# Fewer filler products in attention, five tied behind the state space stage's last products, and the branch gates' products later in the filler

## The chip, the cores and the metric

One core of a Trainium2 chip runs the kernel. The metric is the device time of one execution in microseconds (us). Three runs of the kernel before gave 1414.95, 1415.39 and 1415.87 us; the median is 1415.39 us.

## What is computed

One layer of an encoder with four mixers side by side, for 1024 tokens of width 1024, all in 32-bit floats. Cut to what matters here:

```python
hn = rms_norm(x, norm_scale)
a_x, a_g, q, k, v, b_g, c_x, c_g, d_x, d_g, merge = split(hn @ w_in)   # ten of width 512, merge of 4096
y_a = rglru_mixer(a_x, ...) * silu(a_g)                # gated linear recurrence, both directions
y_b = neighbourhood_attention(q, k, v, ...) * silu(b_g)
y_c = s5_mixer(c_x, ...) * silu(c_g)                   # complex state space, then gelu and a GLU
y_d = pool_mixer(d_x, ...) * silu(d_g)
gates = sigmoid(merge)                                 # four of width 1024
merged = sum over n of (ys[n] @ w_branch[n]) * gates[n]
x = x + merged @ w_out
x = x + sigmoid(x @ ple_gate) * (p @ ple_proj)
```

## The kernel before

Each big product is made of three: both operands are split into a high part (a rounded copy, by ScalarE, ACT) and a low part (the rest, by VectorE, DVE), and `mm3` (L88) multiplies high by high, low by high and high by low into one PSUM tile. A **piece** of `hn @ w_in` gives 128 columns of z for 512 tokens: 8 blocks of the inner dimension by three, 24 matmuls of 128x512 on TensorE (PE). In the trace these are the matmuls of `hnH` or `hnL` with `wh` or `wl`. A new block of 128 columns serves two pieces and needs one split, `wh` on ACT and `wl` on DVE; a new load of 1 MB (`wr`) serves four.

The program runs in stages: start (norms, the per-layer embedding's product), attention, the state space stage (`s5`, L927), its GLU (`glu`, L1099), the gated recurrence (`lru`), pooling, the merge of the four branches, and the two last products (`final`). The stages up to the recurrence leave PE free at times, and for that there is a **filler**: a generator of 108 pieces (`fill`, made in `run`, L1308), which are handed out in a fixed order of parts. A part is four pieces per 256 columns; it brings a function that consumes the result: `gates` (16 pieces each, a sigmoid on ACT and a write to DRAM), `branch_gate` (8 each, a sigmoid on ACT, a multiplication on DVE into `bgt`, and a write), `pool_part` (8, a copy), `s5_u` (4, a copy).

How much filler each stage gets is set by hand. In `attention` (L382) the loop over units of the rounds calls `next(side)`; from the middle of the second round on `side` is the filler. In the stages behind it `drive` (L188) runs the main generator, adds up what it says of PE and DVE, the latter times a factor of `SC`, and takes a piece whenever PE's sum is the smaller. Between `s5` and `glu` two pieces are taken outright.

This is the order in which the program is written down. The order that the engines run is made by a scheduler, which goes through the written order with a timeline of its own and may bring an instruction forward where its engine would be idle; the pieces' buffers (three for `wh` and `wl`, two for `wr`, in turn) and PSUM tiles bound how far. Each engine then runs its list in order.

The state space stage goes through four batches of 128 channels (`s5_batch`, L937), each in two halves `h`. In a batch DVE makes tables (`Gf`, `Q`, `E`), PE transposes `Gf` into `Gt`, and then for each half: PE's V products (`ps_s<-U,Gt`, L1043), DVE's products with `E` into `vr` and `vi`, four scans into `xs`, products into `Xr` and `Xi`, and PE's Y products (`U,M`, then `Xr,Q` and `Xi,Q`, L1089 and L1091), which ACT copies to `Y`. `vr` and `Xr` are one buffer, so the next half's `vr` waits for the Y products. Behind the last half `Y` goes to DRAM (`ydr`), comes back as `gy`, passes a gelu on ACT and DVE, is split into `ygH` and `ygL`, and GLU's products begin.

The change touches `mm3`, `z_gen` (L157), the loop of `attention`, the two lines of products in `s5_batch`, and `run`. `behind` (L704) is there before: it ties an instruction's place in the order behind another's, with no wait.

Of the kernel before, what the change touches and what calls it, by code (L numbers as in the profile page):

```python
# [24 lines left out]
BANDS = (0, 8, 24, 32)  # L25
SC = (1.15, 1.35, 0.95)
VIDX = (0, 1, 1, 2)


class Kern:  # L30
    def __init__(self, tc, es, ins, out):
# [9 lines left out]
        self.dp = es.enter_context(tc.tile_pool(name="dp", bufs=1, space=DRAM))  # L41
        self.zt = "zz"
        self.gd = {}
        self.sgd = {}
# [43 lines left out]
    def mm3(self, ps, pairs):  # L88

        n = len(pairs)  # L90
        mm = self.nc.tensor.matmul
        for k, (aH, aL, bH, bL) in enumerate(pairs):
            mm(ps, aH, bH, start=(k == 0), stop=False)  # L93
            mm(ps, aH, bL, start=False, stop=False)  # L94
            mm(ps, aL, bH, start=False, stop=(k == n - 1))  # L95

    def tr(self, ps, src, k):
# [59 lines left out]
    def z_gen(self, parts):  # L157
# [15 lines left out]
        for k in range(len(todo)):  # L173
            if k + 1 < len(todo):
                prep(k + 1)
            H, L, ct, f = ready.pop(0)
            for hf in range(2):
                ps = self.ps(self.zt[hf])
                t = slice(hf * 512, hf * 512 + 512)
                self.mm3(ps, [(H[:, k, :], L[:, k, :], self.hnH[k][:, t], self.hnL[k][:, t])  # L180
                              for k in range(8)])
                yield 5.2, 0.55 + (f(ct, hf, ps) or 0.0)
# [199 lines left out]
    def attention(self, ap, fill):  # L382
        nc = self.nc
# [19 lines left out]
        side = self.z_gen([self.s5_u(0)])  # L403
        for rd in range(4):
# [5 lines left out]
            for u, _ in enumerate(self.at_units(ap, rd, qk, bias, vd)):  # L410
                if rd < 2 and side is not fill or u % 4 != 2:
                    next(side, None)
                if rd == 0 and u == 1:
                    raw1 = self.qk_load(1)
                if u == 3:
                    next(prep, None)
                    if rd == 0:
                        side = self.at_z(1, raw1)
                        zq = zq + next(side)
                    if rd == 1:  # L420
                        side = fill
# [515 lines left out]
    def s5_batch(self, sb, ct):  # L937
        nc = self.nc
# [15 lines left out]
        Gt = []  # L954
# [82 lines left out]
        for h in range(2):  # L1037
            gg = slice(h * 4, h * 4 + 4)
            V = []
            for k in range(2):  # L1040
                pv = self.ps("s")
                for g in range(4):
                    nc.tensor.matmul(pv[:, g * 128:g * 128 + 128], Gt[k][:, h * 4 + g, :], U[:, h * 4 + g, :],  # L1043
                                     start=True, stop=True)
                V.append(pv)
# [40 lines left out]
            for g in range(4):  # L1086
                c = slice(g * 128, g * 128 + 128)
                a = h * 4 + g
                nc.tensor.matmul(py[:, c], M[:, a, :], U[:, a, :], start=True, stop=False)  # L1089
                for k in range(2):  # L1090
                    nc.tensor.matmul(py[:, c], Q[k][:, a, 1:9, :].rearrange("p t c -> p (t c)"), X[k][:, c],  # L1091
                                     start=False, stop=(k == 1))
            self.copy_a(Y[:, gg, :], py.rearrange("p (g j) -> p g j", g=4))
# [214 lines left out]
    def run(self):  # L1308
        tc = self.tc
        with tc.tile_pool(name="gzp", bufs=2, reuse_waits="tile") as self.gzp:  # L1310
            fill = self.z_gen([self.s5_u(1), self.branch_gate(2, 3584), self.gates(1), self.branch_gate(0, 512), self.branch_gate(3, 4608), self.branch_gate(1, 2560), self.gates(3), self.gates(2), self.pool_part(), self.gates(0)])
            with tc.tile_pool(name="zp", bufs=1, reuse_waits="tile") as self.zp:
# [3 lines left out]
            self.drive(self.s5(), fill, SC[0])  # L1316
            next(fill)
            next(fill)
            self.zt = "zt"
            self.drive(self.glu(), fill, SC[1])  # L1320
            with tc.tile_pool(name="pu", bufs=1, reuse_waits="tile") as pu:
# [50 lines left out]
```

## Time and profile before

| | |
|---|---|
| three runs, median (lowest to highest) | 1415.39 us (1414.95 to 1415.87) |
| the profiled execution, its own time | 1414.34 us |
| its span, first to last instruction | 1412.5 us |
| PE busy | 1366.8 us, 97% |
| PE's weight loads busy | 1120.5 us, 79% |
| DVE busy | 842.0 us, 60% |
| ACT busy | 559.0 us, 40% |
| mean granted TensorE clock | 0.989 |

The profile is of one execution. The span starts at its first instruction; 1.84 us of the execution's time lie around it. Matmuls are pipelined and their ends are modelled: a matmul of 128x512 is shown with some 0.39 us, and the next one starts 0.23 us behind it, so that a busy PE is not PE at its peak, and the pace is read from starts. The clock is given as a share of 2.4 GHz; it has two levels, 1.00 and 0.50. A wait is put down to what ended it last.

### The profile page before, as it was taken

What the parts mean: (1) busy time and instruction counts of PE and PEld (TensorE: products, weight loads), DVE (VectorE), ACT (ScalarE), POOL (GpSimd) and SP (SyncE); (2) the same over time, 40 slices, a digit from 0 to 9 for tenths busy, and PEclk for the clock granted to TensorE, in tenths of its full rate; (3) what the DMA queues carried; (4) which work ended last, traced back from release to release, by engine and by line L of the source; (5) the groups of instructions that cost most, each with busy time, mean ns of one, the idle gap of its engine ahead of it and who ended that gap; (6) DMA issues with size and microseconds to landing.
All of it is one profiled execution on the core that took longest, in us unless ns stands there. A gap on an engine that the chain in (4) does not pass through costs nothing.

```text
span 1412.5 us, 18099 instructions
## 1 busy us (share of the span) xinstructions
PE 1366.8 (97%) x6876; PEld 1120.5 (79%) x6876; DVE 842.0 (60%) x1593; ACT 559.0 (40%) x861; POOL 19.6 (1%) x79
## 2 busy tenths in 40 slices
PE   8999999999999999999839999999999999999998
PEld 6888888888888878888727777778888888888886
DVE  6373446554369797979757447265457766722332
ACT  6344655878622122221133846747322212211221
POOL 2100000000000000000000000000000000000000
PEclk9999999999999999999959999999999999999999
DMA  9533323244243233332344133231846655324443
GB/s 318 162 92 97 119 68 96 87 125 131 73 121 109 90 114 100 105 95 74 108 134 141 49 120 109 74 105 55 321 167 210 210 197 173 127 97 150 171 141 119
DMA packets 134840, 181.91 MB, mean 129 GB/s; under 512 B 29120, under 2 KB 92632, under 8 KB 134754
## 3 DMA queue, kind: packets, MB, share of 16 engines
q1 hardware_dynamic: 134338, 180.72, 40.1%
q8 instruction: 54, 0.88, 0.3%
q14 instruction: 32, 0.26, 0.1%
q0 software_dynamic: 416, 0.04, 0.0%
HBM read 127.06 MB, written 54.03 MB: 128 GB/s over the span
## 4 chain that ended last, share of the span: by engine, by line
PE 92%; DVE 4%; ACT 2%; DMA 1%; issue 1%; SPq 0%; ACTq 0%
PE ps_z L93 19%; PE ps_z L94 19%; PE ps_z L95 19%; PE ps_t L98 4%; PE ps_t L93 3%; PE ps_t L94 3%; PE ps_t L95 3%; PE ps_s L94 2%; PE ps_o L94 2%; PE ps_s L95 2%; PE ps_o L95 2%; PE ps_s L93 2%; PE ps_o L93 2%; PE ps_o L584 2%; PE ps_s L549 2%; PE ps_s L1091 1%
## 5 line engine op out<-in xcount | busy, mean ns | idle before, releaser
L93 PE MATMUL ps_z<-hnH,wh 128*128 128x512 f32 x736 | 290.8, 395 | 3.8 <-DVE xs L1071 1.8
L95 PE MATMUL ps_z<-hnH,wl 128*128 128x512 f32 x736 | 288.6, 392 | 1.7 <-DVE wl L65 1.7
L94 PE MATMUL ps_z<-hnL,wh 128*128 128x512 f32 x736 | 289.6, 393 | 0.0
L93 PEld LDWEIGHTS ps_z<-hnH,wh 128*128 128x128 f32 x736 | 138.2, 188 | 34.8 <-issue 2.4
L95 PEld LDWEIGHTS ps_z<-hnH,wl 128*128 128x128 f32 x736 | 138.3, 188 | 30.0 <-DVE wl L65 2.1
L94 PEld LDWEIGHTS ps_z<-hnL,wh 128*128 128x128 f32 x736 | 138.3, 188 | 27.6 <-issue 1.2
L65 DVE TENSOR_TENSOR wl<-wr,wh 128x1024 fp32r<-128x1024 f32 x88 | 107.3, 1223 | 83.1 <-ACT wh L81 61.0
L81 ACT ACTIVATE wh<-wr 128x1024 fp32r<-128x1024 f32 x88 | 92.8, 1057 | 113.4 <-PE ps_z L94 66.8
L93 PE MATMUL ps_t<-hnH,wh 128*128 128x512 f32 x224 | 87.9, 393 | 0.0
L94 PE MATMUL ps_t<-hnL,wh 128*128 128x512 f32 x224 | 87.8, 392 | 0.0
L95 PE MATMUL ps_t<-hnH,wl 128*128 128x512 f32 x224 | 87.5, 391 | 0.0
L93 PE MATMUL ps_z<-wh,hnH 128*128 128x512 f32 x192 | 75.6, 395 | 0.3 <-ACT zqk L81 0.3
L94 PE MATMUL ps_z<-wl,hnH 128*128 128x512 f32 x192 | 75.1, 393 | 0.0
L95 PE MATMUL ps_z<-wh,hnL 128*128 128x512 f32 x192 | 74.6, 395 | 0.0
L555 DVE CUSTOM_DVE_ANT_0 sc<-ps_s,bias 128x384 f32<-128x384 f32 x64 | 33.9, 555 | 49.0 <-PE ps_s L549 42.3
L77 ACT ACT_TABLE_LOAD x47 | 60.3, 1283 | 3.8 <-issue 2.9
L95 PE MATMUL ps_z<-wh,mL 128*128 128x512 f32 x128 | 51.0, 398 | 0.0
L94 PE MATMUL ps_o<-myL,wh 128*128 128x512 f32 x128 | 50.5, 395 | 0.0
L95 PE MATMUL ps_o<-myH,wl 128*128 128x512 f32 x128 | 50.5, 395 | 0.0
L93 PE MATMUL ps_s<-myH,wh 128*128 128x512 f32 x128 | 50.5, 395 | 0.0
L95 PE MATMUL ps_s<-myH,wl 128*128 128x512 f32 x128 | 50.5, 395 | 0.0
L93 PE MATMUL ps_o<-myH,wh 128*128 128x512 f32 x128 | 50.5, 394 | 0.0
(382 smaller groups left out, 2590.4 us busy)
## 6 DMA issues: line engine op xcount, KB each, us to landing
wr<-in_w_in_dram SPq DMA_DIRECT2D x32, 1024.0 KB, 5.7
gd<-gz SPq DMA_DIRECT2D x32, 512.0 KB, 3.1
mgt<-gd SPq DMA_DIRECT2D x32, 512.0 KB, 3.6
sg<-bgt SPq DMA_DIRECT2D x16, 512.0 KB, 2.9
my<-yd SPq DMA_DIRECT2D x16, 512.0 KB, 3.5
mbr<-in_w_branch_dram SPq DMA_DIRECT2D x8, 1024.0 KB, 7.1
bias<-E SPq DMA_DIRECT2D x128, 48.0 KB, 2.0
xt<-in_x_dram SPq DMA_DIRECT2D x8, 512.0 KB, 10.0
```

What stands on the lines that cost most here:

```text
L65: self.nc.vector.tensor_tensor(out, a, b, ALU.subtract)
L77: self.nc.scalar.activation(out, a, f, **kw)
L81: return self.nc.scalar.activation(out, a, AF.Copy)
L93: mm(ps, aH, bH, start=(k == 0), stop=False)
L94: mm(ps, aH, bL, start=False, stop=False)
L95: mm(ps, aL, bH, start=False, stop=(k == n - 1))
L98: self.nc.tensor.transpose(ps, src, self.ident[:k, :k])
L549: nc.tensor.matmul(pss[h], q[h][:, qs], km[h][(slice(0, 128),) + ks], start=(p == 0), stop=(p == 1))
L555: nc.vector.tensor_tensor_reduce(sc, pss[h], bias[g][h][:, VIDX[j], :], 1.0, -3e38, ALU.add, ALU.max, mx)
L584: m = self.nc.tensor.matmul(po[64 * h:64 * h + 64, j * 128:j * 128 + 128], vb[:, g + c, j, h * 64:h * 64 + 64], PT[h][:, c * 128:c * 128 + ...
L1091: nc.tensor.matmul(py[:, c], Q[k][:, a, 1:9, :].rearrange("p t c -> p (t c)"), X[k][:, c], start=False, stop=(k == 1))
```

## The change

It changes four things. Attention hands out filler in every other unit wherever its `side` is the filler (before: in three of four). The factor of the state space stage, `SC[0]`, goes from 1.15 to 1.25. Behind `s5`, five pieces are taken outright instead of two; the first matmul of two of them is tied behind the last V product of the last batch, that of the other three behind its last Y product. And in the filler's order of parts, three branch gates (0, 3 and 1) move behind `gates(3)` and `gates(2)`.

```diff
-SC = (1.15, 1.35, 0.95)
+SC = (1.25, 1.35, 0.95)
...
     def mm3(self, ps, pairs):
...
         for k, (aH, aL, bH, bL) in enumerate(pairs):
-            mm(ps, aH, bH, start=(k == 0), stop=False)
+            i = mm(ps, aH, bH, start=(k == 0), stop=False)
+            first = i if k == 0 else first
...
+        return first
...
     def z_gen(self, parts):
...
-                self.mm3(ps, [(H[:, k, :], L[:, k, :], self.hnH[k][:, t], self.hnL[k][:, t])
-                              for k in range(8)])
+                first = self.mm3(ps, [(H[:, k, :], L[:, k, :], self.hnH[k][:, t], self.hnL[k][:, t])
+                                      for k in range(8)])
+                if self.hold is not None:
+                    self.behind(first, self.hold)
                 yield 5.2, 0.55 + (f(ct, hf, ps) or 0.0)
...
     def attention(self, ap, fill):
...
-                if rd < 2 and side is not fill or u % 4 != 2:
+                if side is not fill or u % 2:
                     next(side, None)
...
     def s5_batch(self, sb, ct):
...
-                    nc.tensor.matmul(pv[:, g * 128:g * 128 + 128], Gt[k][:, h * 4 + g, :], U[:, h * 4 + g, :],
-                                     start=True, stop=True)
+                    self.last_v = nc.tensor.matmul(pv[:, g * 128:g * 128 + 128], Gt[k][:, h * 4 + g, :],
+                                                   U[:, h * 4 + g, :], start=True, stop=True)
...
-                    nc.tensor.matmul(py[:, c], Q[k][:, a, 1:9, :].rearrange("p t c -> p (t c)"), X[k][:, c],
-                                     start=False, stop=(k == 1))
+                    self.last_y = nc.tensor.matmul(py[:, c], Q[k][:, a, 1:9, :].rearrange("p t c -> p (t c)"),
+                                                   X[k][:, c], start=False, stop=(k == 1))
...
     def run(self):
...
-            fill = self.z_gen([self.s5_u(1), self.branch_gate(2, 3584), self.gates(1), self.branch_gate(0, 512), self.branch_gate(3, 4608), self.branch_gate(1, 2560), self.gates(3), self.gates(2), self.pool_part(), self.gates(0)])
+            fill = self.z_gen([self.s5_u(1), self.branch_gate(2, 3584), self.gates(1), self.gates(3), self.gates(2),
+                               self.branch_gate(0, 512), self.branch_gate(3, 4608), self.branch_gate(1, 2560),
+                               self.pool_part(), self.gates(0)])
...
             self.drive(self.s5(), fill, SC[0])
-            next(fill)
-            next(fill)
             self.zt = "zt"
+            for self.hold, n in ((self.last_v, 2), (self.last_y, 3)):
+                for _ in range(n):
+                    next(fill)
+            self.hold = None
             self.drive(self.glu(), fill, SC[1])
```

The orders of the engines show where the pieces go. All counts of pieces here are of matmuls of `hnH`, `hnL` with `wh`, `wl`, by 24; there are 120 of them in all, before and after (the filler's 108 and 12 of the state space input and the recurrence). In attention, 24.75 pieces stand ahead of the last value product (`ps_o<-PT,vb`) before and 24.25 after.

On PE, the end of the Y products of the third batch's first half (`Q_5509` before, `Q_5378` after), which is where 61.96 pieces have gone by before and 59.00 after. Before:

```order
L1089 MATMUL ps_s<-U,M 128x128
L1091 MATMUL ps_s<-Xr,Q_5508 128x128
L1091 MATMUL ps_s<-Xi,Q_5509 128x128
L95 MATMUL ps_z<-hnH,wl 128x512
L93 MATMUL ps_z<-hnH,wh 128x512
L94 MATMUL ps_z<-hnL,wh 128x512
L95 MATMUL ps_z<-hnH,wl 128x512
```

and after:

```order
L1094 MATMUL ps_s<-U,M 128x128
L1096 MATMUL ps_s<-Xr,Q_5377 128x128
L1096 MATMUL ps_s<-Xi,Q_5378 128x128
L1048 MATMUL ps_s<-U,Gt_5364 128x128 x4
L1094 MATMUL ps_s<-U,M 128x128
L1096 MATMUL ps_s<-Xr,Q_5377 128x128
L101 MATMUL ps_t<-ident,Gf_5898 128x128 x8
L1096 MATMUL ps_s<-Xi,Q_5378 128x128
```

The filler's matmuls that followed are gone. From here to the last V product of the fourth batch 10.0 pieces stand on PE before and none after; the second half of the third batch and the fourth batch's transposes, `Q,Bb` products and first half follow each other.

On PE, the last V product of the fourth batch, tied to by the first two pieces. Before, the last V product (`Gt_6095`) is followed at once by the last half's Y products; after:

```order
L1096 MATMUL ps_s<-Xi,Q_5968 128x128
L1048 MATMUL ps_s<-U,Gt_5954 128x128 x4
L94 MATMUL ps_t<-hnH,wh 128x512
L96 MATMUL ps_t<-hnL,wh 128x512
L97 MATMUL ps_t<-hnH,wl 128x512
L94 MATMUL ps_t<-hnH,wh 128x512
```

Two pieces now stand between the last V product and the last half's `Xr` product: 61.00 pieces have gone by when the Y products run, where it was 72.00.

On PE, the end of the last Y products. Before, GLU's first products follow:

```order
L1089 MATMUL ps_s<-U,M 128x128
L1091 MATMUL ps_s<-Xr,Q_6108 128x128
L1091 MATMUL ps_s<-Xi,Q_6109 128x128
L93 MATMUL ps_s<-ygH_6634,wh 128x512
L93 MATMUL ps_o<-ygH_6634,wh 128x512
```

and after:

```order
L1094 MATMUL ps_s<-U,M 128x128
L1096 MATMUL ps_s<-Xr,Q_5967 128x128
L1096 MATMUL ps_s<-Xi,Q_5968 128x128
L94 MATMUL ps_t<-hnH,wh 128x512
L96 MATMUL ps_t<-hnL,wh 128x512
L97 MATMUL ps_t<-hnH,wl 128x512
```

Ten pieces, the three tied ones among them, now stand between the last Y product and GLU's first product, which comes when 71.00 have gone by. From GLU's last product on, 48 pieces are left before and 47 after. On DVE, none of the 24 multiplications into `bgt` that stood in the state space stage is left there, and 18 splits `wl` stand in it where there were 21: 17 for 18 up to the third batch's first Xi, one for three behind it.

## Rows read from the trace of the kernel before

**Rows 1.** The page, part 2: busy tenths of 40 slices of 35.3 us, and the granted clock.

```profile
PE   8999999999999999999839999999999999999998
...
DVE  6373446554369797979757447265457766722332
...
PEclk9999999999999999999959999999999999999999
```

**Rows 2.** PE's longest waits: engine, tile, line, what ended them; us, times, longest.

```profile
PE ps_s L93 <- ACT ygH L82: 16.5, 1, 16.5
PE ps_s L1091 <- DVE Xr L65: 9.3, 1, 9.3
```

**Rows 3.** PE's timeline, third batch's Y products, and the gap: start, length, operation, idle before.

```profile
629.37 0.38 PE L1091 MATMUL ps_s<-Xi,Q 128*128 128x128 f32 x2
...
699.48 1.05 PE L1043 MATMUL ps_s<-U,Gt 128*128 128x128 f32 x8
...
711.76 0.80 PE L1091 MATMUL ps_s<-Xr,Q 128*128 128x128 f32 x2 [9.30 <-DVE Xr L65]
...
717.21 0.64 PE L1091 MATMUL ps_s<-Xi,Q 128*128 128x128 f32 x2
734.30 0.79 PE L93 MATMUL ps_s<-ygH,wh 128*128 128x512 f32 x1 [16.45 <-ACT ygH L82]
```

**Rows 4.** Stretches: us, busy PE, PE's weight loads, DVE, ACT, POOL; clock, DMA share, GB/s.

```profile
392.60:626.70 234.10, 231.41 (x1300) 191.53 (x1299) 204.40 (x473) 56.17 (x87) 0.00 (x0) 1.00 0.37 106
626.70:713.20 86.50, 75.08 (x447) 63.07 (x445) 67.53 (x125) 15.08 (x25) 0.00 (x0) 0.95 0.27 81
629.40:700.30 70.90, 70.90 (x430) 59.99 (x428) 55.38 (x105) 15.08 (x25) 0.00 (x0) 1.00 0.31 92
...
734.00:738.40 4.40, 4.10 (x10) 3.00 (x11) 4.38 (x6) 3.33 (x5) 0.00 (x0) 0.50 0.41 148
```

**Rows 5.** PE's timeline, inside a filler piece in the state space stage.

```profile
431.71 0.39 PE L94 MATMUL ps_z<-hnL,wh 128*128 128x512 f32 x1
...
432.39 0.39 PE L94 MATMUL ps_z<-hnL,wh 128*128 128x512 f32 x1
```

**Rows 6.** DVE's waits from 392 to 627 us.

```profile
DVE wl L65 <- ACT wh L81: 7.2, 4, 3.2
DVE vr L59 <- PE ps_s L1091: 5.7, 2, 3.7
DVE bgt L59 <- ACT bgt L77: 4.5, 3, 3.2
...
DVE vt L59 <- PE ps_s L1043: 2.0, 2, 1.6
```

**Rows 7.** DVE's waits from 627 to 714 us, all of them.

```profile
DVE vr L59 <- PE ps_s L1091: 8.7, 2, 4.9
DVE vt L59 <- PE ps_s L1043: 8.0, 2, 4.3
```

**Rows 8.** DVE's timeline, the halves of the third and fourth batch.

```profile
631.57 0.69 DVE L59 TENSOR_TENSOR vr<-ps_s,E 128x512 f32<-128x512 f32 x1 [4.87 <-PE ps_s L1091]
...
637.73 0.69 DVE L59 TENSOR_TENSOR vt<-ps_s,E 128x512 f32<-128x512 f32 x1 [4.33 <-PE ps_s L1043]
...
696.22 0.69 DVE L59 TENSOR_TENSOR vr<-ps_s,E 128x512 f32<-128x512 f32 x1 [3.84 <-PE ps_s L1091]
700.56 0.69 DVE L59 TENSOR_TENSOR vt<-ps_s,E 128x512 f32<-128x512 f32 x1 [3.65 <-PE ps_s L1043]
...
712.47 0.69 DVE L62 TENSOR_TENSOR Xi<-Xi,vt 128x512 f32<-128x512 f32 x1
```

**Rows 9.** DVE's groups from 392 to 627 us: busy us, mean ns, idle before them.

```profile
L65 DVE TENSOR_TENSOR wl<-wr,wh 128x1024 fp32r<-128x1024 f32 x18 | 22.0, 1222 | 7.4 <-ACT wh L81 7.2
L59 DVE TENSOR_TENSOR bgt<-bgt,ps_z 128x512 f32<-128x512 f32 x24 | 16.4, 682 | 4.5 <-ACT bgt L77 4.5
```

**Rows 10.** ACT's timeline, the last copy of Y products.

```profile
717.88 0.60 ACT L81 ACTIVATE Y<-ps_s 128x512 f32<-128x512 f32 x1 [17.61 <-PE ps_s L1091]
```

More of the change, by code (lines that the diff above doesn't have):

```diff
@@ L1316, in run @@
             self.drive(self.s5(), fill, SC[0])
-            next(fill)
-            next(fill)
             self.zt = "zt"
+            for self.hold, n in ((self.last_v, 2), (self.last_y, 3)):
+                for _ in range(n):
+                    next(fill)
+            self.hold = None
             self.drive(self.glu(), fill, SC[1])
```

## The prediction

> **What bounds the kernel now.** I read the page first. In 40 slices PE is at 9 nearly everywhere; one slice, the twenty-first, shows 3, and the granted clock 5 of 10 there [rows 1]. So PE's work sets the time, and little but that one hole can be won. Who PE waits for comes next [rows 2]: 16.5 us before the first product of the gate behind the state space stage (GLU for short), for ygH; 9.3 us before the state space stage's last Y products, for Xr. PE's timeline there [rows 3] shows the order of events: the last V product at 699.48, the last half's Y products from 711.76 to 717.85 (0.43 us from one instruction to the next), then nothing until 734.30. The stretches [rows 4] give the clock: 0.50 from 734 to 738.4, where ten matmuls took 4.1 us, so behind the gap PE is at 1.2 GHz, having done nothing for 16 us. A filler piece fills PE for 24 matmuls; three take 0.68 us from start to start [rows 5], so a piece is 5.44 us. Five pieces are 27.2 us, and the two waits together 25.8 us: the size of the change's idea is right.
>
> But what stands ahead of the hole matters more. Up to the third batch's first half DVE is at work 204.40 of 234.10 us while PE shows 231.41 [rows 4]; both are nearly full there. What DVE waits for in it is small and mixed [rows 6]: 5.7 us before vr and 2.0 us before vt, for PE; 7.2 us and 4.5 us before the filler's own wl and bgt, for ACT. Behind that point it waits only before vr and vt, 8.7 and 8.0 us in two halves' turns [rows 7].
>
> **What the orders say.** Not what the code's numbers suggest. In attention the order holds half a piece less than before, not five: what attention no longer asks for, the scheduler brings forward from the state space stage. The five held pieces are what it can no longer bring forward. Before, 72 pieces stand ahead of the last Y product; now 61. And those 61 are so spent that from the third batch's first Y products to the last V product there are none, where there were 10. Behind the last Y product stand 10 pieces in a row, where there were none.
>
> **The sum.** Everything behind the last Y product is PE's work, in the same amount but for those pieces. So the time is the end of the last Y product, plus what PE has left then.
>
> *What is left then.* 11 pieces more, 11 x 5.44 = 59.8 us. The gap goes: 16.45 us of waiting, and the slow start, 4.1 us for ten matmuls that take 10 x 0.227 = 2.3 us at full clock, 1.8 us. GLU's chain (last product to first ygH, 16.5 us) lies behind 54.4 us of filler, with sigmoids and splits between it on ACT and DVE; even at twice its length it is hidden. So 59.8 - 18.3 = 41.5 us more. **If the last Y product does not end 41.5 us earlier than at 717.85, the kernel is slower.** That is the point of decision: 676.3 us.
>
> *When the third batch's first Y products run.* By PE: 59.0 pieces stand ahead of the Xi product, where 61.96 did; 2.96 x 5.44 = 16.1 us less. It ran at 629.37 [rows 3], and vr, which waits for the Y products behind it, at 631.57 [rows 8]; now 613.3 and 615.5. By DVE: it starts the stage at 392.6, now 2.7 us earlier (half a piece), at 389.9. To the end of Xi were 234.1 us [rows 4]. Out go the 24 multiplications of branch gates, 0.682 us each, 16.4 us [rows 9], their 4.5 us of waits, and one split of 18 (1.22 us). That leaves 212.0. But these filled some of DVE's waiting for PE: in the first two batches vr and vt show 7.7 us, in the last two, which have no gate's work, 16.7. With nothing to fill them they should cost there what they cost in the last two, 9.0 us more: 389.9 + 212.0 + 9.0 = 610.9, against 626.7. PE is the later by a little, so vr starts at 615.5, 16.1 us earlier.
>
> *The rest of the stage.* From vr to the end of the last Xi are 713.16 - 631.57 = 81.6 us [rows 8]. It is DVE's chain: 67.53 us of work in 86.5 [rows 4]; PE's filler only fits around it. Two of its three splits move out, 2.4 us. The waits shorten, as no filler lies between Y products and the next V product, but they do not vanish: the Y products, the ACT copy that frees their PSUM buffer and the V product remain. The third batch's wait before vt, 4.33 us, falls to the copy and the product, 0.6 + 1.05 us [rows 3, 10] less the 0.6 that DVE works meanwhile, with a handover some 1.3 us. In the fourth, PE has idled and runs at half clock: 3.84 before vr stays some 3.5, and 3.65 before vt falls to 2.2. Together 4.8 us: 81.6 - 2.4 - 4.8 = 74.4, so Xi ends at 689.9. The two held pieces lie under 11.2 us of DVE (vt at 700.56 to Xr at 711.76), 12.4 with a split that now stands there. They are 10.9 us at 2.4 GHz and 21.8 at 1.2. PE comes from idling, and the Y products behind the 9.3 us wait ran at half pace to their end at 717.85 [rows 3], as did ten of GLU's, behind 16 us of nothing [rows 4]. I take 14, and give the last products 3 us instead of 4.7: 692.9.
>
> So the stage ends 25.0 us earlier, not 41.5, and the kernel is 16.5 us slower: 1414.34 + 16.5 = 1430.9 us. The profiled execution lies 1.05 us below the median of the three runs, 1415.39; I leave that in the range. In other words: for 70.9 us PE was full [rows 4], 54.4 us of it filler. That filler is taken out and DVE saves some 8 us there, so PE idles about 45 us ahead of the place where it used to idle 27.
>
> What I cost at nothing: the held pieces' ties (order on one engine, no semaphore); the later branch gates' 24 multiplications, since DVE's slices behind the stage show 2 to 7 with PE at 9 [rows 1]; the SP queue, where two GLU loads now stand behind a filler's gate write, some 11 us behind the last Y product. If that cover is short, GLU is later, under 54.4 us of filler still.
>
> **Who binds, by a rule.** By PE's busy share, 231.41 of 234.10, PE binds the stage, and 11 pieces less would end it 59.8 us earlier. The Trainium skill, "Perfetto Trace Analysis", section "Identifying the Most-Contended Engine", holds that matmul busy time is a poor measure, and has TensorE judged by the busy share of its weight loads, against occupancy for VectorE. By it the stretch reads 191.53 for the weight loads and 204.40 for DVE [rows 4], so DVE is the more contended, and taking work from PE gives nothing. The trace agrees only in part, since DVE has waits for PE in the same stretch. The sum by the first reading is the first rival's; by the rule it is near the forecast.
>
> **The rivals.**
> *PE binds to the end (faster).* DVE's waits would all be PE's lateness and go with the filler. Then the last Y product ends at 717.85, less 59.8, less PE's idle time up to there (2.7 us of the 234.1 and 11.4 of the 86.5 [rows 4]) and 2.7 us of slow products: 641.2. The time is 1414.34 - 76.6 + 41.5 = 1379 us. For it speaks PE's full row, 70.90 of 70.90. Against it: in the stretch from 626.70 DVE works 67.53 us, and even without a single wait it cannot end before 615.5 + 74.4 - 7.0 = 682.9. It decides from 676.3 on. Chance 0.08, with all that lies between.
> *The waits vanish, and so does the loss (about the same).* Without the 7.0 us of waits that I leave in the rest of the stage it is 1424; to reach 1418 or less, DVE must also be 6 us faster in the first two batches and attention end earlier than half a piece. 0.06.
> *Slower by more.* The held pieces run all at half clock, 21.8 us instead of 14 (7.8 us); the waits of the rest of the stage stay as they were (4.8); attention, with its own work placed tighter, ends no earlier (2.7): 1446 us. Ten pieces in a row ahead of GLU may also make the recurrent stage late. 0.08 for more than that.
> *The change doesn't do what it says.* For attention this is so, by the orders, and is in the sum; the ties do hold.
>
> **How the numbers follow.** Forecast, between 1418 and 1446: 0.78. The three cases above take 0.22. The range reaches from 1415, where the first two rivals begin, to 1446. A measurement of this kernel can tell about 0.2%, 2.8 us, from no change. Faster by more than that 0.09, within it 0.06, slower 0.85.
>
> **What would show it.** In the profile after: PE's busy share falls to a few tenths in two or three slices near 620 to 690 us, and the clock's row shows 5 to 7 there; the wait for ygH is gone; PE's waits in the state space stage sum to some 45 us, for Gf, Q, E or Xr; DVE's row stays at 8 or 9; the last Y product ends at 693 (676 would be break-even); ten pieces run behind it without a hole; the recurrent stage and the merge keep PE at 9. The forecast is wrong if DVE's own pace in the fourth batch is quicker than its 67.53 us of work say, or if PE starves elsewhere.

## The result and the profile after

The changed kernel takes **1438.18 us** (median of four runs, 1438.04 to 1438.61), the kernel before beside it 1415.29 us (1414.95 to 1415.87). The ratio is 1.0162, with a 95% interval of 1.0144 to 1.0179: slower by 22.9 us. The forecast was 1430.9 us, in a range of 1415 to 1446. The profiled execution is one of the four, 1438.21 us with a span of 1436.4 us; 1.8 us lie around it, as before.

The page of the kernel after, part 2, in 40 slices of 35.9 us (compare [rows 1]):

```profile
PE   8999999999999999945999999999999999999998
...
DVE  6374446564289797987544373662748767723332
...
PEclk9999999999999999976999999999999999999999
```

Before, one slice of PE stood at 3. Now two stand at 4 and 5, from 610 to 682 us, and the granted clock is down in both. PE's longest waits in the kernel after, by engine, tile, line and what ended them (us, times, longest; compare [rows 2]):

```profile
PE ps_s L1096 <- DVE Xr L66: 13.9, 3, 9.6
PE ps_s L1094 <- DMA M<-kd: 11.2, 1, 11.2
PE ps_s L1001 <- DVE Q L66: 6.7, 2, 4.3
PE ps_z L94 <- ACT wh L82: 4.7, 4, 1.4
PE ps_z L97 <- DVE wl L66: 3.5, 3, 2.1
```

The 16.5 us before ygH are gone. What has come instead are waits of the state space stage: for Xr, for M (a table of each batch, which goes through DRAM) and for Q. PE's timeline shows where they lie (start, length, operation, idle before; compare [rows 3]):

```profile
614.49 0.39 PE L1096 MATMUL ps_s<-Xi,Q 128*128 128x128 f32 x2
...
628.21 0.79 PE L1096 MATMUL ps_s<-Xr,Q 128*128 128x128 f32 x2 [9.56 <-DVE Xr L66]
...
660.81 0.77 PE L1094 MATMUL ps_s<-U,M 128*128 128x128 f32 x2 [11.17 <-DMA M<-kd]
...
676.02 0.77 PE L94 MATMUL ps_t<-hnH,wh 128*128 128x512 f32 x1
...
688.74 0.49 PE L1096 MATMUL ps_s<-Xr,Q 128*128 128x128 f32 x2 [0.18 <-DVE Xr L66]
...
692.30 0.39 PE L1096 MATMUL ps_s<-Xi,Q 128*128 128x128 f32 x2
692.45 0.48 PE L94 MATMUL ps_t<-hnH,wh 128*128 128x512 f32 x1
...
746.98 0.39 PE L94 MATMUL ps_s<-ygH,wh 128*128 128x512 f32 x1
```

The third batch's first Y products end at 614.9; the next filler matmul is the tied one at 676.02. In between PE has only the stage's own products, and waits ahead of each group of them. From 692.45 to 746.98 ten pieces run without a hole. The same in stretches (us, then busy PE, weight loads, DVE, ACT, POOL; clock, DMA share, GB/s; compare [rows 4]):

```profile
392.20:612.30 220.10, 220.10 (x1253) 182.79 (x1251) 188.88 (x448) 53.72 (x83) 0.00 (x0) 1.00 0.36 105
614.70:690.10 75.40, 36.56 (x222) 30.54 (x220) 65.04 (x122) 7.99 (x14) 0.00 (x0) 0.71 0.14 37
650.00:660.00 10.00, 0.00 (x0) 0.00 (x0) 9.66 (x17) 0.00 (x0) 0.00 (x0) 0.73 0.28 65
692.70:746.90 54.20, 54.20 (x240) 44.85 (x240) 23.60 (x23) 22.35 (x27) 0.35 (x6) 1.00 0.53 175
```

From 614.70 to 690.10 PE is at work 36.56 of 75.40 us and DVE 65.04. DVE's timeline has the first and the last instruction of that stretch (compare [rows 8]):

```profile
614.69 0.69 DVE L60 TENSOR_TENSOR vr<-ps_s,E 128x512 f32<-128x512 f32 x1 [2.37 <-PE ps_s L1096]
...
689.45 0.69 DVE L63 TENSOR_TENSOR Xi<-Xi,vt 128x512 f32<-128x512 f32 x1
```

To compare many kernels I use one more number, worked out from the trace: **the time lost on PE**. For each matmul it is the time to the start of the next one, less the median of that time for the same kind of matmul in the trace of before. It holds waits and slow clock together. Summed over the execution it is 64.4 us before and 88.3 after; the difference, 23.9 us, is that of the spans, 1436.4 - 1412.5. By stretches:

| lost on PE, us | before | after |
|---|---|---|
| start and attention | 10.9 | 13.2 |
| state space stage, to the last V product | 12.1 | 54.6 |
| last half's Y products, and up to GLU | 29.6 | 2.9 |
| GLU | 2.9 | 1.0 |
| recurrence | 7.2 | 13.2 |
| behind it: last filler, merge, final | 1.7 | 3.4 |

The change does what it was written for: 26.7 us less are lost around the gap. It pays 42.5 us for that ahead of the last V product, and 10.0 us in three other places (2.3 up to attention's end, 6.0 in the recurrence, 1.7 behind it); GLU gives 1.9 back.

### The profile page after: what moved, and what is told of

Its sections match the earlier page's. It is cut to its first block, busy times and chain, and to the rows that moved or that the text cites. A ratio compares the mean times of both kernels' runs of the same rounds, so it can differ in the third digit from the quotient of the medians.

```text
span 1436.4 us, 18095 instructions
## 1 busy us (share of the span) xinstructions
PE 1375.5 (96%) x6876; PEld 1127.5 (78%) x6876; DVE 842.7 (59%) x1593; ACT 559.2 (39%) x861; POOL 19.9 (1%) x79
## 4 chain that ended last, share of the span: by engine, by line
PE 86%; DVE 7%; ACT 5%; issue 1%; DMA 1%; SPq 0%; ACTq 0%; DVEq 0%
PE ps_z L94 18%; PE ps_z L97 18%; PE ps_z L96 18%; PE ps_t L101 4%; PE ps_t L94 3%; PE ps_t L96 3%; PE ps_t L97 3%; PE ps_s L94 2%; PE ps_s L96 2%; PE ps_s L97 2%; PE ps_o L94 2%; PE ps_o L96 2%; PE ps_o L97 2%; PE ps_s L554 2%; PE ps_o L589 2%; ACT sg L78 1%
## 5 line engine op out<-in xcount | busy, mean ns | idle before, releaser
L94 PE MATMUL ps_z<-hnH,wh 128*128 128x512 f32 x712 | 281.7, 396 | 3.2 <-ACT wh L82 3.2
L97 PE MATMUL ps_z<-hnH,wl 128*128 128x512 f32 x712 | 280.6, 394 | 3.6 <-DVE wl L66 3.5
L96 PE MATMUL ps_z<-hnL,wh 128*128 128x512 f32 x712 | 279.9, 393 | 0.0
L82 ACT ACTIVATE wh<-wr 128x1024 fp32r<-128x1024 f32 x88 | 93.0, 1057 | 138.3 <-PE ps_z L96 55.8
L94 PE MATMUL ps_t<-hnH,wh 128*128 128x512 f32 x248 | 97.7, 394 | 0.0
L96 PE MATMUL ps_t<-hnL,wh 128*128 128x512 f32 x248 | 97.1, 392 | 0.0
L97 PE MATMUL ps_t<-hnH,wl 128*128 128x512 f32 x248 | 96.9, 391 | 0.0
L78 ACT ACTIVATE gz<-ps_z 128x512 f32<-128x512 f32 x53 | 31.3, 590 | 93.1 <-issue 71.4
L560 DVE CUSTOM_DVE_ANT_0 sc<-ps_s,bias 128x384 f32<-128x384 f32 x64 | 34.2, 555 | 48.5 <-PE ps_s L554 38.7
L94 PEld LDWEIGHTS ps_t<-hnH,wh 128*128 128x128 f32 x248 | 46.9, 189 | 11.1 <-issue 1.1
L97 PEld LDWEIGHTS ps_t<-hnH,wl 128*128 128x128 f32 x248 | 46.9, 189 | 10.0 <-issue 0.2
L96 PEld LDWEIGHTS ps_t<-hnL,wh 128*128 128x128 f32 x248 | 46.9, 189 | 9.9 <-issue 0.4
```

What stands on the lines that cost most here:

```text
L78: self.nc.scalar.activation(out, a, f, **kw)
L82: return self.nc.scalar.activation(out, a, AF.Copy)
L94: i = mm(ps, aH, bH, start=(k == 0), stop=False)
L560: nc.vector.tensor_tensor_reduce(sc, pss[h], bias[g][h][:, VIDX[j], :], 1.0, -3e38, ALU.add, ALU.max, mx)
```

## The experiments

Twelve kernels ran, each compared with the kernel before on the same chip (1414.8 to 1415.0 us). My theory was that the ties alone make the loss: tied pieces cannot be brought forward into the end of the stage, which lasts for DVE's chain, so PE idles there. The rivals were that the new order of parts costs it, through the branch gates that now lie in the recurrence, or that attention's number does.

This table is the base for all of them. Counts are of pieces, by the order of PE's list: ahead of the last V product; between the last Y product and GLU; from GLU's end to the recurrence's; behind it. What a row lacks of 120 stands between the last V and the last Y product, two pieces in each kernel with ties, or inside GLU. Then the end of the last Y product, the lost time of the stretches above, and the median in us. The lost time is that of one profiled execution, which can lie some us from the median.

| kernel | to V | to GLU | recurr. | behind | last Y ends | start, att. | to last V | gap | GLU | recurr. | behind | median |
|---|---|---|---|---|---|---|---|---|---|---|---|---|
| before | 72.0 | 0 | 33.0 | 15.0 | 717.8 | 10.9 | 12.1 | 29.6 | 2.9 | 7.2 | 1.7 | 1415.3 |
| after | 59.0 | 10 | 35.0 | 12.0 | 692.7 | 13.2 | 54.6 | 2.9 | 1.0 | 13.2 | 3.4 | 1438.2 |
| e1 no tie | 68.2 | 1.9 | 35.0 | 12.0 | 710.1 | 13.2 | 19.6 | 6.0 | 9.9 | 13.3 | 3.4 | 1415.3 |
| e2 order only | 70.0 | 0 | 35.2 | 14.8 | 709.0 | 11.6 | 13.4 | 29.8 | 2.5 | 17.0 | 1.6 | 1425.2 |
| e3 old order | 62.0 | 9 | 33.0 | 12.0 | 708.1 | 12.3 | 55.8 | 1.7 | 1.0 | 14.2 | 3.1 | 1439.1 |
| e4 factor 1.45 | 69.0 | 10 | 33.1 | 3.9 | 701.7 | 12.6 | 9.2 | 3.4 | 1.0 | 13.3 | 24.1 | 1416.5 |
| e5 ties only | 62.0 | 9 | 33.0 | 12.0 | 708.1 | 12.1 | 55.9 | 1.7 | 1.0 | 14.0 | 3.6 | 1439.0 |
| e6 old numbers | 59.0 | 10 | 35.0 | 12.0 | 697.0 | 12.3 | 58.5 | 4.4 | 1.0 | 14.1 | 3.5 | 1443.9 |
| e7 1.45, GLU 0.5 | 69.0 | 6 | 34.2 | 8.8 | 704.0 | 12.8 | 9.2 | 6.3 | 3.3 | 13.6 | 12.9 | 1405.5 |
| e8 before, 1.30 | 69.0 | 7 | 33.0 | 9.0 | 717.5 | 11.0 | 26.1 | 4.5 | -0.1 | 7.2 | 11.8 | 1409.5 |
| e9 1.42 | 67.0 | 5 | 35.0 | 11.0 | 702.4 | 12.7 | 20.7 | 3.5 | 0.3 | 16.8 | 4.5 | 1408.4 |
| e10 old order | 67.0 | 5 | 33.0 | 13.0 | 712.6 | 12.5 | 31.7 | 2.9 | 0.3 | 7.2 | 2.7 | 1408.3 |
| e11 lru 0.9 | 67.0 | 5 | 33.0 | 13.0 | 703.8 | 13.3 | 19.9 | 5.0 | 0.2 | 10.2 | 3.2 | 1402.9 |
| e12 | 69.0 | 5 | 31.0 | 13.0 | 703.9 | 13.4 | 9.2 | 4.9 | -0.1 | 11.0 | 3.0 | 1391.5 |

### e1: without the tie

```diff
-                if self.hold is not None:
-                    self.behind(first, self.hold)
```

> The change with the five pieces still taken behind the state space stage, but not tied; all else as changed. By the written order of PE's list 71.1 pieces then stand ahead of the last Y product (61.0 with the ties, 72.0 before) and two behind it. My theory (the ties starve PE in the part of the stage that lasts for DVE's chain): PE's idle time of some 39 us in the stage goes, the last Y product ends at 708 to 716, two pieces (10.9 us) lie in the gap before GLU, of which 5 to 6 us stay, and the time is 1402 to 1410 us, below the kernel before. Rival (the later branch gates, or the attention's number, are what costs): the time stays at 1430 us or more, and the waits are found behind 780 us.

Measured: 1415.29 us, ratio 1.0005 (0.9996 to 1.0015). The rival falls: without the tie the 23 us are gone, though attention's number, the factor and the new order are all still there. But it should have been faster than before, and is not. PE's longest waits in this kernel:

```profile
PE ps_s L1094 <- DVE Xr L66: 6.9, 1, 6.9
PE ps_s L94 <- ACT ygH L83: 6.7, 2, 5.6
PE ps_z L94 <- ACT wh L82: 4.2, 4, 1.4
PE ps_z L97 <- DVE wl L66: 3.3, 2, 2.1
```

The stage and the gap lose 25.6 us where they lost 41.7, and of the gap before ygH 5.6 us stay, as expected. What was won went elsewhere: GLU itself loses 7.0 us more than before, the recurrence 6.1, and the rest 4.0. My sum had only the two waits in it.

### e2: the new order of parts alone

```diff
-            fill = self.z_gen([self.s5_u(1), self.branch_gate(2, 3584), self.gates(1), self.branch_gate(0, 512), self.branch_gate(3, 4608), self.branch_gate(1, 2560), self.gates(3), self.gates(2), self.pool_part(), self.gates(0)])
+            fill = self.z_gen([self.s5_u(1), self.branch_gate(2, 3584), self.gates(1), self.gates(3), self.gates(2),
+                               self.branch_gate(0, 512), self.branch_gate(3, 4608), self.branch_gate(1, 2560),
+                               self.pool_part(), self.gates(0)])
```

> The kernel before with nothing changed but the filler's order of parts (branch gates 0, 3 and 1 behind gates(3) and gates(2)). 70.0 pieces stand ahead of the last Y product and none between it and GLU. My theory: PE binds the stage with so many pieces, so DVE's 16.4 us of multiplications that move out buy little there; the gap of 16.5 us before ygH stays; 1410 to 1418 us, and if the branch gates are what makes the recurrence stage wait, some 5 us of waits for wl and wh appear behind 780 us. Rival (the order of parts costs the 23 us): 1430 us or more.

Measured: 1425.19 us, ratio 1.0071 (1.0056 to 1.0086): above my range and below the rival's. The stage loses what it lost before (13.4 us to the last V product, 29.8 around the gap). Its last Y product ends 8.8 us earlier, but two pieces, 10.9 us, less stand ahead of it and are left for later: with PE nearly full, DVE's 16.4 us less buy nothing for the total. The recurrence loses 17.0 us where it lost 7.2. That is 9.8 of the 10.4 us by which it is slower than the kernel before beside it.

### e3: the change with the old order of parts

```diff
-            fill = self.z_gen([self.s5_u(1), self.branch_gate(2, 3584), self.gates(1), self.gates(3), self.gates(2),
-                               self.branch_gate(0, 512), self.branch_gate(3, 4608), self.branch_gate(1, 2560),
-                               self.pool_part(), self.gates(0)])
+            fill = self.z_gen([self.s5_u(1), self.branch_gate(2, 3584), self.gates(1), self.branch_gate(0, 512), self.branch_gate(3, 4608), self.branch_gate(1, 2560), self.gates(3), self.gates(2), self.pool_part(), self.gates(0)])
```

> The change with the filler's old order of parts; ties, attention and factor as changed. 64.0 pieces stand ahead of the last Y product, 11 between it and GLU's last start. My theory: DVE's chain binds the stage and has its 24 multiplications back (16.4 us, some of it in waits): the last Y product ends at 702 to 708 instead of 692.7; three pieces fewer are left behind it (16.3 us), and without the branch gates the recurrence loses some 5 us of waits: 1427 to 1435 us. If the 7.6 us that I missed behind the stage do not come from the branch gates, the upper end. Rival (the order of parts costs, the ties do not): 1415 us or less.

Measured: 1439.11 us, ratio 1.0170 (1.0154 to 1.0185), some 4 us above the top of my range. In the stage it is as I said: the last Y product ends at 708.1 instead of 692.7, and three pieces more stand ahead of it. 15.4 us later, 16.3 us less to do: in this kernel, where PE idles in the stage with either order, the branch gates' place is worth nothing to the total. But the recurrence still loses 14.2 us, though the branch gates are out of it. So the branch gates are not the whole cause of the time that I missed there.

### e4: more pieces inside the stage

```diff
-SC = (1.25, 1.35, 0.95)
+SC = (1.45, 1.35, 0.95)
```

> The change with the state space stage's factor at 1.45 instead of 1.25, so that more pieces are written down inside the stage and the ties keep only the last ones from being brought forward. 69.0 pieces stand ahead of the last V product (59.0 in the change), two tied ones between it and the last Y products, 10 behind them. My theory: PE is full again up to the last V product, the last Y product ends at 700 to 712, the gap is gone: 1392 to 1402 us, faster than both kernels by 1 to 1.6 per cent. Rival (held pieces or the ties as such cost, by the clock or by DVE's waits for the Y products): 1415 us or more.

Measured: 1416.48 us, ratio 1.0014 (1.0004 to 1.0024). Against the change that is 21.7 us faster, and the place is the one I named: to the last V product PE loses 9.2 us instead of 54.6, and the last Y product ends at 701.7. Ten pieces more, 54.4 us of PE's work, made that end 9.0 us later. But the kernel is not faster than before. By the number alone the rival (1415 us or more) has it; the table says otherwise, since the stage and the gap lose 12.6 us where they lost 41.7 before, so that the ties as such do not cost. This wait shows where the time went:

```profile
PE ps_s L94 <- ACT myH L82: 16.1, 1, 16.1
```

`myH` is the split operand of the merge's first product. It hangs on the last of the recurrence, and the filler behind the recurrence used to cover it: 15.0 pieces before, 12.0 in the change, 3.9 here. The stretches from the recurrence's last product to the merge's first, and from there to the end (columns as above) show the hole, and the clock at 0.83 of full:

```profile
996.90:1034.40 37.50, 21.43 (x95) 17.38 (x94) 23.77 (x21) 20.68 (x24) 0.00 (x0) 0.83 0.31 109
1034.40:1406.60 372.20, 369.99 (x1624) 301.27 (x1624) 206.79 (x265) 79.33 (x92) 0.00 (x0) 0.99 0.51 176
```

So there is a third place of waiting that neither the change nor my prediction had in view. It is covered in the kernel before, and of the ten pieces that the stage got here 8.1 come from there.

### e5: the ties alone

The edits of `mm3`, `z_gen` and `s5_batch` as in the change, and in `run`:

```diff
-            next(fill)
-            next(fill)
             self.zt = "zt"
+            for self.hold, n in ((self.last_v, 2), (self.last_y, 3)):
+                for _ in range(n):
+                    next(fill)
+            self.hold = None
```

`SC`, attention and the order of parts stay as before.

> The kernel before with only the five pieces tied behind the state space stage (two behind the last V product, three behind the last Y product); attention's number, the factor and the order of parts as before. 62.0 pieces stand ahead of the last V product, as with the change under the old order of parts. My theory (the ties alone make the loss): PE idles some 38 us ahead of the last V product, the gap before ygH is gone, and the time is 1435 to 1441 us. Rival (the loss needs the attention's number or the factor as well): within 5 us of the kernel before, 1410 to 1420 us.

Measured: 1438.96 us, ratio 1.0173 (1.0157 to 1.0188). PE's longest waits:

```profile
PE ps_s L1096 <- DVE Xr L66: 13.7, 2, 9.6
PE ps_s L1094 <- DMA M<-kd: 11.2, 1, 11.2
PE ps_s L1001 <- DVE Q L66: 6.8, 2, 4.1
```

The same waits as after the whole change, and much the same loss ahead of the last V product, 55.9 us for 54.6. With e1 this settles it from both sides: the ties make the slowdown without the other three edits, and with those three but without the ties it is not there. (That five pieces are taken instead of two, behind the line with `zt` instead of ahead of it, is so in e1 too.) Which of the two ties does it, the one behind the last V product or the one behind the last Y product, no run separates.

### e6: attention's number and the factor as before

```diff
-SC = (1.25, 1.35, 0.95)
+SC = (1.15, 1.35, 0.95)
...
-                if side is not fill or u % 2:
+                if rd < 2 and side is not fill or u % 4 != 2:
```

> The change with attention's handing out and the stage's factor as before (1.15); ties and new order of parts stay. 24.75 pieces stand in attention (24.25 in the change), 59.0 ahead of the last V product, 61.0 ahead of the last Y product, as in the change. My theory (these two numbers move half a piece and nothing else): the change's own time within 4 us, 1434 to 1442 us. Rival (fewer pieces in attention starve it, and part of the 23 us goes there): 1425 to 1432 us.

Measured: 1443.85 us, ratio 1.0202 (1.0185 to 1.0219), 1.9 us above my bound and 5.7 above the change. The place is the same, the size is not nothing. With half a piece more in attention the last value product comes 1.8 us later, the last V product 3.0 and the last Y product 4.3. DVE's chain starts behind attention, and what delays it there is not given back. It also grows on the way: DVE's waits before vr and vt, for PE, sum to 25.5 us in this stage and to 19.0 in the change's. What makes them longer is not shown.

### e7: fewer pieces for GLU

```diff
-SC = (1.25, 1.35, 0.95)
+SC = (1.45, 0.5, 0.95)
```

> The change with the state space stage's factor at 1.45 (as in the run with that alone) and GLU's factor at 0.5 instead of 1.35. 69.0 pieces stand ahead of the last V product, two between it and the last Y products, 6 behind them instead of 10, and 9 behind the recurrence instead of 4. My theory now (a piece is worth its time only where PE's own work waits, and there are three such places: the stage's end, GLU's start and the merge's start, which waited 16.1 us for myH with 4 pieces left): the merge's wait goes and nothing opens elsewhere, 1390 to 1400 us. Rival (the pieces taken from GLU's start open its gap of 16.5 us again, or the merge waits for something that does not depend on the pieces): 1405 us or more.

Measured: 1405.53 us, ratio 0.9936 (0.9922 to 0.9951): faster than before, and 11 us faster than e4 by the medians (the spans of the two profiled executions lie 5.6 us apart, since e4's is the quickest of its runs and this one the slowest of its own). The merge gains 11.2 us, 12.9 lost behind the recurrence instead of 24.1, and the rival has a part in it too: with 6 pieces ahead of GLU instead of 10, the gap and GLU lose 5.2 us more. The merge's wait has not gone, so I was too hopeful. With 8.8 pieces the waits for `myH`, `myL` and `wl` are 5.5 us together, and the slow clock behind them (0.88 from 1023.9 to 1065.0) does the rest.

### e8: ties with the old order and the old attention

Against e5:

```diff
-SC = (1.15, 1.35, 0.95)
+SC = (1.3, 0.8, 0.95)
```

> The kernel before with the five tied pieces, the stage's factor at 1.30 instead of 1.15 and GLU's at 0.8 instead of 1.35; attention and order of parts as before. 69.0 pieces stand ahead of the last V product (62.0 with the ties alone), two between it and the last Y products, 7 behind them, 9 behind the recurrence. My theory (the ties are harmless once enough pieces are written down ahead of them, and the order of parts matters little): 1388 to 1400 us. Rival (only the new order of parts lets DVE finish the stage early enough for this): 1405 us or more, with the loss inside the stage.

Measured: 1409.53 us, ratio 0.9962 (0.9949 to 0.9975). With the factor raised the ties no longer make the kernel slower than before. But by number and place this is the rival's side: the stage loses 26.1 us where the new order (e7, same 69.0 pieces) loses 9.2, and ends 13.5 us later. So when PE is nearly full, the branch gates' place does matter to the stage. The recurrence, on the other hand, loses only 7.2 us here.

### e9, e10, e11: three kernels side by side

All have two and two pieces tied and GLU's factor at 0.5; e9 `SC = (1.42, 0.5, 0.95)`, e10 `SC = (1.35, 0.5, 0.95)` with the old order of parts, e11 `SC = (1.42, 0.5, 0.9)`.

```diff
-            for self.hold, n in ((self.last_v, 2), (self.last_y, 3)):
+            for self.hold, n in ((self.last_v, 2), (self.last_y, 2)):
```

> The change with the stage's factor at 1.42, GLU's at 0.5, and two pieces instead of three behind the last Y product. 67.0 pieces stand ahead of the last V product, 69.0 ahead of the last Y product, 5 behind it, 78.42 ahead of the recurrence's first product, 11 behind its last. For the time: the three places of waiting (stage's end, GLU's start, merge's start) are all covered, and 1390 to 1402 us is expected; if the merge's start needs more than 11 pieces, 1403 to 1408 us. For the 6 us that the recurrence lost in the change: so far the stretch lost 13 to 14 us where an odd number of pieces (77.83, 79.83, 81.83) stood ahead of its first product, and 7 where an even one did with the old order of parts (76.42, 82.42). If the position decides (my theory now), it loses 7 us here. If the new order of parts decides, 13 to 17 us.

> The old order of parts with the change's attention; factor 1.35, GLU's 0.5, two and two pieces tied: by count the same places as the run beside it (67.0 ahead of the last V product, 69.0, 74.0, 78.42 ahead of the recurrence, 13 behind it). My theory: DVE has its 24 multiplications of branch gates in the stage, so the last Y product ends 8 to 14 us later than in the run beside it and PE idles there instead; the recurrence loses 7 us; 1398 to 1408 us, 5 to 12 us slower than the run beside it. Rival (PE binds the stage with either order): the same time within 3 us.

> As the first run of this call, with the recurrence's factor at 0.9 instead of 0.95: 13 pieces stand behind the recurrence instead of 11. If the merge's first products wait for myH because too little filler is left (my theory), the merge's loss, 12.8 us with 9 pieces left, is 3 us here, and the recurrence has enough with two fewer: 1388 to 1400 us. If the recurrence needs them, its loss grows by up to 10.9 us, and the time is that of the first run or above.

Measured: e9 1408.44 us, ratio 0.9956 (0.9944 to 0.9969); e10 1408.33, 0.9955 (0.9943 to 0.9968); e11 1402.90, 0.9917 (0.9903 to 0.9931).

e9 and e10 have the same counts up to the recurrence, and differ in the order of parts. The stage goes as expected: the last Y product 10.2 us later with the old order. I expected e10 slower by 5 to 12 us, and it is not, since its recurrence loses 9.6 us less. That is the rival's number (within 3 us) without its reason: to the last V product e10 loses 11.0 us more. PE's waits in the recurrence's stretch, first e9:

```profile
PE ps_z L97 <- DVE wl L66: 5.4, 2, 3.3
PE ps_z L94 <- ACT wh L82: 1.4, 2, 1.1
```

then e10:

```profile
PE ps_z L97 <- DVE wl L66: 1.6, 1, 1.6
PE ps_z L94 <- ACT wh L82: 1.1, 1, 1.1
```

My theory of the position (odd or even number of whole pieces ahead of the recurrence's first product) is only half of it: with e9 the number is even, and 16.8 us are lost. Where it is odd (77.83, 79.83, 81.83 or 87.83), the stretch loses 13.2 to 14.2 us in all seven kernels, with either order of parts. Where it is even, the old order loses 7.2 us (before, e8, e10) and the new one 10.2 to 17.0 (e2, e9, e11, e12). So neither decides alone, and why it is so stays open. What the loss consists of is seen in the trace of after. PE around 838 us:

```profile
838.25 0.50 PE L94 MATMUL ps_z<-hnH,wh 128*128 128x512 f32 x1 [1.40 <-ACT wh L82]
...
841.13 0.51 PE L97 MATMUL ps_z<-hnH,wl 128*128 128x512 f32 x1 [2.15 <-DVE wl L66]
...
842.90 0.63 PE L97 MATMUL ps_z<-hnH,wl 128*128 128x512 f32 x1
```

and ACT just ahead:

```profile
834.32 1.38 ACT L78 ACTIVATE sg<-ps_o,gb 64x512 f32<-64x512 f32 x2
835.73 1.39 ACT L78 ACTIVATE sg<-ps_s,gb 64x512 f32<-64x512 f32 x2
837.14 1.06 ACT L82 ACTIVATE wh<-wr 128x1024 fp32r<-128x1024 f32 x1
```

A piece needs a new block of weights; its split `wh` stands on ACT behind sigmoids of the recurrence (`sg`), and `wl` follows on DVE. PE waits twice, 1.40 and 2.15 us, and from 842.3 us to 845.7 the granted clock is 0.50, with 0.63 us for a matmul. The waits and the slow matmuls behind them are what such a meeting of a new block with the recurrence's own work costs.

e11 against e9: two pieces moved from the recurrence to behind it. The merge's loss falls from 4.5 to 3.2 us, and the recurrence's from 16.8 to 10.2: it did not need them there.

### e12: a version that beats both

```diff
-SC = (1.25, 1.35, 0.95)
+SC = (1.45, 0.5, 0.85)
...
-            for self.hold, n in ((self.last_v, 2), (self.last_y, 3)):
+            for self.hold, n in ((self.last_v, 2), (self.last_y, 2)):
```

> The version that should beat both: the change with the stage's factor at 1.45, GLU's at 0.5, the recurrence's at 0.85, and two and two pieces tied. 69.0 pieces stand ahead of the last V product (67.0 in the run before this one), 71.0 ahead of the last Y product, 5 behind it, 80.42 ahead of the recurrence, 13 behind it. My theory (each of the three waiting places needs its pieces, the rest is free to move): the stage loses 9 to 10 us ahead of the last V product instead of 19.9, as in the other two runs with 69.0; the merge loses 3 us as with 13 left; the recurrence, with two pieces fewer than in the run before, loses 10 to 13: 1392 to 1398 us. If the recurrence has too little with 26.6 pieces, its loss grows by up to 10.9 us and the time is 1400 to 1406 us.

Measured: **1391.51 us**, ratio 0.9832 (0.9818 to 0.9845); 23.5 us faster than before and 46.7 faster than the change, just below my range. The page, part 2:

```profile
PE   7999999999999999999999999999999999999998
...
PEclk9999999999999999999999999999999999999999
```

No slice of PE stands below 9 but the first and the last. The stretch that the change left half empty, from the third batch's vr to the end of the last Xi, is in this kernel from 616.2 to 699.9 us, and in it DVE has more of the filler's own work (two of DVE's groups, then the stretch):

```profile
L66 DVE TENSOR_TENSOR wl<-wr,wh 128x1024 fp32r<-128x1024 f32 x6 | 7.3, 1221 | 4.3 <-ACT wh L82 4.3
L60 DVE TENSOR_TENSOR bgt<-bgt,ps_z 128x512 f32<-128x512 f32 x6 | 4.1, 683 | 0.0
```

```profile
616.20:699.90 83.70, 79.29 (x455) 65.92 (x454) 74.21 (x134) 18.40 (x29) 0.00 (x0) 1.00 0.29 88
```

PE works 79.29 of 83.70 us, where the change had 36.56 of 75.40. The stretch is 8.3 us longer for 42.7 us more of PE's work, and DVE has 9.2 us more in it (74.21 for 65.04). So what filler costs here, as long as PE has room, is near what it asks of DVE, the splits and the branch gates' multiplications, and not what it asks of PE.

## Why the prediction was right

Direction and place were right, the size was 16.5 us for 23.9 by the spans. The stage's end came out within 0.2 us; all of the error lies behind it. That it came so close is luck in part: its terms were off by up to 2.3 us each, in both directions, as the next paragraphs show.

**What the orders say** was the step that carried it, and it held: attention's number moved half a piece, the held pieces are what the scheduler could no longer bring forward. e1 and e5 show it apart from everything else: of the 13 pieces that leave the stage ahead of its last V product, ten leave it by the ties alone (e5, 62.0 for 72.0).

**When the third batch's first Y products run.** I had vr start at 615.5; it started at 614.69. One part of the step was off: I let attention end, and DVE start the stage, 2.7 us earlier, and it was 0.4 us (392.2 for 392.6). To the end of Xi it was then 220.1 us instead of the 221.0 I had (212.0 and 9.0 of waits). I had PE as the later of the two by a little; in the trace Xi was ready at 612.3 and its first product started at 612.38, without a wait.

**The rest of the stage.** Xi was to end at 689.9, and ended at 690.1: 75.4 us instead of 74.4. Of the waits, vr had 4.3 us inside this stretch (the 2.37 us before its first vr lie ahead of it) and vt 3.9, 8.2 where I left 7.0. The two held pieces took from 676.02 to 688.6, 12.5 us instead of 14, with only the first few matmuls at half clock; the last products took 3.95 us instead of 3. The last Y product was to end at 692.9, and ended at 692.7. PE's idle time from 614.70 to 690.10 is 75.40 - 36.56 = 38.8 us, where I had some 45; the slower clock, 0.71 in that stretch, comes on top. The longest of PE's waits there, 11.2 us for M, was not among those that I had named.

**What is left then** is the term that was mis-sized. I said 41.5 us more; from the last Y product to the end of the span there were 1436.4 - 692.7 = 743.7 us, where there had been 1412.5 - 717.85 = 694.65: **49.1 us more**. The 59.8 us of pieces, the gap of 16.45 us and GLU's slow start, 1.8 us, are right: GLU and the gap lost as expected. The missing 7.6 us are, by the table of lost time, the recurrence, 6.0 us more, and the stretch behind it, 1.7. I had costed the later branch gates at nothing, since DVE's slices behind the stage show 2 to 7, and said that ten pieces ahead of GLU might make the recurrent stage late, but gave that no size. A share of busy time does not show whether a split comes in time; the waits for `wl` and `wh` in that stretch before (2.8 us) were the row to read. That the branch gates alone are not to blame e3 shows, and why the recurrence loses more stays open.

**The rivals.** That PE binds to the end is refuted by e4 as clearly as by the change: ten pieces more in the stage move the last Y product by 9.0 us and not by 54.4. For the kernel before itself e8 says the same: with the old order and the old attention, three pieces (16.3 us) less ahead of the last V product bring that product's last matmul 0.4 us earlier, 699.83 us for 700.25. By the rule that I had weighed (the Trainium skill, "Perfetto Trace Analysis", "Identifying the Most-Contended Engine") DVE is the contended engine in that stage, and these runs agree: in the change DVE's row reads 65.04 of 75.40 us, the weight loads' 30.54, and what the pieces that e12 has more in it add to its length is near what they add to DVE's work. It is close, though: with DVE's 16.4 us taken out (e2), PE's lost time up to the last V product does not fall (13.4 us for 12.1). The Trainium skill says on the same page, in the section "Optimization Strategy", that a kernel whose most contended engine changes over time may gain by interleaving its regimes. That is what the filler does, and what the ties undid: e12's stretch above and that of the change are the two sides of it.

## What to carry to other kernels

Filler that is free to move has a use at each place where the main work waits, and a piece given to one place is taken from another. Before holding pieces back for a visible gap, count how many pieces each place needs, the covered ones too: here GLU's start was covered with 5, the stage needed some 69 ahead of its last V product (with the new order of parts), and the merge's start some 13. And an order that a scheduler makes is changed by what it may no longer do, not by the number in the code: read the order that comes out before putting a price on the change.

## What had not been expected

- The covered wait at the merge has a steep edge. Lost time behind the recurrence by the pieces left there: 15.0 pieces 1.7 us; 13.0, 2.7 to 3.2; 12.0, 3.1 to 3.6; 11.0, 4.5; 9.0, 11.8; 8.8, 12.9; 3.9, 24.1.
- The clock fell to half behind two short waits, 1.40 and 2.15 us at 838 and 841 us in the recurrence, with a few matmuls between them; the prediction had it only behind long ones.
- The order of the filler's parts moved some 10 us of loss from the state space stage to the recurrence (e9 against e10), with the same total: two effects of one line that cancel, and that only a table by stages shows.
